# Attention scores from queries and keys that are split into two parts where they are projected

## The chip, the cores and the metric

One core of a Trainium2 chip runs the whole kernel. The metric is the device time of one execution in microseconds (us). The engines named below are TensorE (PE, and PEld for its weight loads), VectorE (DVE), ScalarE (ACT), GpSimd (POOL) and SyncE (SP), whose only work here is to issue DMAs.

## What is computed

The kernel is one transformer layer on 1024 tokens of width 1024: two mixers side by side (an attention with latent projections, and an RWKV-7 recurrence), then a mixture of 32 experts. The change is in the attention, whose reference is, cut to what matters:

```python
MLA_HEADS, QK_NOPE_DIM, QK_ROPE_DIM, V_HEAD_DIM = 8, 64, 32, 64   # QK_HEAD_DIM = 96
def mla_group(p, cos, sin, q_norm_g, w_uq, kv_norm_g, w_uk, w_uv, out_g):
    ...
    q = (rms_norm(q_lat, q_norm_g) @ w_uq).reshape(b, s, MLA_HEADS, QK_HEAD_DIM)
    q = jnp.concatenate([q[..., :QK_NOPE_DIM],
                         rope(q[..., QK_NOPE_DIM:], cos[:, :, None, :], sin[:, :, None, :])], axis=-1)
    c_kv = rms_norm(kv_lat, kv_norm_g)
    k_nope = (c_kv @ w_uk).reshape(b, s, MLA_HEADS, QK_NOPE_DIM)
    v = (c_kv @ w_uv).reshape(b, s, MLA_HEADS, V_HEAD_DIM)
    k_rot = rope(k_rot, cos, sin)
    k = jnp.concatenate([k_nope, jnp.broadcast_to(k_rot[:, :, None, :], (b, s, MLA_HEADS, QK_ROPE_DIM))], axis=-1)
    o = causal_attention(q, k, v)
...
def one_block(args):            # in causal_attention, one block of 128 queries
    scores = jnp.einsum('bqhd,bkhd->bhqk', qb, k, preferred_element_type=jnp.float32) * scale
    scores = jnp.where(k_pos[None, :] <= q_pos[:, None], scores, -jnp.inf)
    probs = jax.nn.softmax(scores, axis=-1).astype(v.dtype)
    return jnp.einsum('bqhk,bkhd->bqhd', probs, v)
```

All inputs and the output are float32.

## The kernel before

**Split products.** Most products of the kernel don't multiply float32 directly. `split` (L204) makes two F32R tiles of a float32 one: `hi`, a copy on ScalarE, and `lo`, the difference, on VectorE. `mm` (L189) then runs three passes into one PSUM bank, at lines L193 (hi by hi), L194 and L195 (the two mixed ones). The attention scores are an exception: L892 is one float32 matmul, which shows as two instructions (x2) in the trace.

**The projections** (`phase_c`, L459, about 100 to 345 us). The float32 tiles of 128 x 1024 that pass through this stage come from `stage`, a ring of 3 buffers (L471). `proj` (L425) and `project` (L546) leave their results in two PSUM banks of the tag `sm`, one for each half of the tokens; `sm` has 4 banks. The main loop takes p = 0 to 3 (called pairs below, since each p gives two heads):

- three calls of `shifted`, which fill one `stage` buffer each with r, k and v of the recurrence and write it to `rkv_d`;
- for p = 0 and 2 `rotary` (L556), which makes the rotated rows of four heads in two `stage` buffers t1 and t2 and writes t1 to `q_d` in four DMAs (L565);
- `nope` (L567) twice, for the 64 unrotated rows of q and of k: one `stage` buffer, two ScalarE copies out of PSUM, two DMAs (L572) to `q_d` or `k_d`;
- two products with `uv` that give the values, copied out (L593) and written to `v_d` (L594).

Between them the loop takes pieces of other work: rows of the adaLN modulation (`mod`, DMAs at L384) and normalized residual rows (`xr`, L410 and L414). After pair 2 the first steps of a recurrence unit are put in.

**The mixers** (`mixers`, L951, about 345 to 820 us) run the eight attention heads beside the units of the recurrence: `head(u)` is a generator that gives way after blocks of queries, and `go(u)` takes one more step of unit u. `mla_setup` (L853) makes two persistent pairs of tiles Q and K, for even and for odd heads, of 128 partitions, of which 96 to 127 are set to zero by four memsets on POOL and 64 to 95 of K hold the rotated key `kr_d`, loaded once. `head` (L870) loads Q and the unrotated part of K in two DMAs (L876, L877), and then, for each of 8 blocks of 128 queries, computes the scores against the keys up to the diagonal in stretches of at most 512 columns (`ms`, 3 banks), adds the mask by a small bf16 matmul (L894), takes the maximum on VectorE, the exponential on ScalarE, and multiplies by the values. So a head has scores of 128, 256, 384 and 512 columns for blocks 0 to 3, and for blocks 4 to 7 one of 512 and one of 128, 256, 384 and 512.

**The order of the work.** The program's text doesn't fix it. The kernel is built with `TileContext(nc, schedule_with_timeline_sim=True)` (L1798): a scheduler places the instructions on each engine's queue, from dependences, buffers and its own estimate of times, and an engine then runs its queue in order. All DMAs named here are issued from SP's queue, in order, and an instruction of SP that waits for data or for a free buffer holds up those behind it.

**The experts** (about 1000 to 2460 us) follow; in them the change moves nothing on TensorE.

The lines that matter for the steps are L471 (ring), L556 to L572 (`rotary`, `nope`), L853 to L877 (`mla_setup`, loads of a head) and L892 (score).

Of the kernel before, what the change touches and what calls it, by code (L numbers as in the profile page):

```python
# [10 lines left out]
F32 = mybir.dt.float32  # L11
F32R = mybir.dt.float32r
# [7 lines left out]
P = 128  # L20
T = 1024
# [142 lines left out]
class Build:  # L164
# [49 lines left out]
    def setup(self):  # L214
        nc, tc, ctx = self.nc, self.tc, self.ctx
        cp = self.cp = ctx.enter_context(tc.tile_pool(name="const", bufs=1))
        self.vecs = cp.tile([P, NV], F32, name="vecs")
        nc.sync.dma_start(self.vecs, self.i["vec"])
        self.csts = cp.tile([P, NC_ALL], F32, name="csts")
        nc.scalar.dma_start(self.csts, self.i["cst"][:, 0:NC_ALL])  # L220
        self.ident = self.cst("ident")
        self.ones = cp.tile([P, P], F32, name="ones")
        nc.vector.memset(self.ones, 1.0)
        eps = cp.tile([P, 4], F32, name="eps")
        for j, v in enumerate((1e-5, 1e-6, 64e-5, 1e-24)):
            nc.gpsimd.memset(eps[:, j:j + 1], v)
        self.eps_ln, self.eps_rms, self.eps_gn, self.eps_kk = (eps[:, j:j + 1] for j in range(4))
        self.dx = ctx.enter_context(tc.tile_pool(name="dram", bufs=1, space=bass.MemoryType.DRAM))
        dram = lambda n, sh: self.dx.tile(sh, F32, name=n)

        self.h2_d = dram("h2_d", [T + P, D])
        self.y_d = dram("y_d", [T + P, D])
        self.mod_d = dram("mod_d", [4, D])
        self.rkv_d = dram("rkv_d", [4, 3, P, T])
        self.sg_d = dram("sg_d", [NB, P, 512])
        self.q_d = dram("q_d", [NH, 96, T])
        self.k_d = dram("k_d", [NH, 64, T])
        self.kr_d = dram("kr_d", [32, T])
        self.v_d = dram("v_d", [NB, P, 512])
        self.ab_d, self.t0_d, self.t0t_d = ([dram(f"{n}{u}", [16, 4160]) for u in range(2)] for n in ("ab_d", "t0_d", "t0t_d"))  # L240
        self.xr_d = dram("xr_d", [T, D])
        self.bs_d = dram("bs_d", [NE, 8, 512])
        self.stats = cp.tile([P, NB, 2], F32, name="stats")
# [215 lines left out]
    def phase_c(self, st, keep, rw_stack):  # L459
# [50 lines left out]
        for h, sl in enumerate(halves):  # L510
            V.tensor_mul(t1[0:32, sl], pp[h][0:32], cos[0:32, sl])
            V.tensor_mul(t2[0:32, sl], pp[h][32:64], sin[0:32, sl])
            V.tensor_add(t1[0:32, sl], t1[0:32, sl], t2[0:32, sl])
        nc.sync.dma_start(self.kr_d, t1[0:32])
        norm(slice(2, 3), "kvg", 128)
        qn, kn = nrm[0:2], nrm[2]
        mod()
# [38 lines left out]
        def rotary(g):  # L556
            pr = project("w_uq", 512 + g * P, qn)
            pw = project("w_uq", 768 + g * P, qn)
            t1, t2 = stage(), stage()
            for h, sl in enumerate(halves):  # L560
                V.tensor_mul(t1[:, sl], pr[h], cos[:, sl])
                V.tensor_mul(t2[:, sl], pw[h], sin[:, sl])
                V.tensor_add(t1[:, sl], t1[:, sl], t2[:, sl])
            for j in range(4):
                nc.sync.dma_start(self.q_d[4 * g + j, 64:96], t1[32 * j:32 * j + 32])  # L565

        def nope(name, p, srcs, dst):  # L567
            t = stage()
            for h, pq in enumerate(project(name, p * P, srcs)):
                S.copy(t[:, halves[h]], pq)  # L570
            for h in range(2):
                nc.sync.dma_start(dst[2 * p + h, 0:64], t[h * 64:h * 64 + 64])  # L572

        uv = self.split_tile(wp, [P, 512], "uv")
        wv = stage()[:, 0:512]
# [2 lines left out]
        for p in range(4):  # L578
# [16 lines left out]
            if p == EARLY_UNIT:  # L595
                for _ in (*mods, *xrows):
                    pass
                smr.close()
                self.rw = self.pool(rw_stack, "rw")
                self.unit_consts()  # L600
                self.unit(0)


    def psum(self, tag, bufs):
# [248 lines left out]
    def mla_setup(self, st):  # L853
        nc = self.nc
        kp = self.pool(st, "kp", side="right")
        self.ap = self.pool(st, "ap", bufs=2, side="right")

        self.Q, self.K = ([kp.tile([P, T], F32, name=f"{n}{j}") for j in range(2)] for n in "QK")
        for t in self.Q + self.K:
            nc.gpsimd.memset(t[96:P], 0.0)  # L860
        for K in self.K:
            nc.sync.dma_start(K[64:96], self.kr_d)
        self.nmask = kp.tile([P, P], BF16, name="nmask")
        self.identb = kp.tile([P, P], BF16, name="identb")
        nc.vector.tensor_copy(self.identb, self.ident)
        nc.gpsimd.memset(self.nmask, 0.0)
        nc.gpsimd.affine_select(self.nmask, self.nmask, [[-1, P]], ALU.is_ge, NEG, base=0, channel_multiplier=1)
        self.vp = None

    def head(self, h, oT):  # L870
# [1 line left out]
        nc, ap = self.nc, self.ap  # L872
        V, S, mm = nc.vector, nc.scalar, nc.tensor.matmul
        half, other = (slice(64 * j, 64 * j + 64) for j in (h % 2, 1 - h % 2))
        Q, K = self.Q[h % 2], self.K[h % 2]
        nc.sync.dma_start(Q[0:96], self.q_d[h])  # L876
        nc.sync.dma_start(K[0:64], self.k_d[h])  # L877
        if h % 2 == 0:
            self.vp = ap.tile([P, NB, P], F32, name="vp", bufs=1)
            nc.sync.dma_start(self.vp, self.v_d[:, :, h * 64:h * 64 + P].rearrange("b p c -> p b c"))  # L880
# [2 lines left out]
        for qb in range(NB):  # L883
# [4 lines left out]
            for j, c in enumerate(range(0, n, 512)):  # L888
                w = min(n - c, 512)
                s = self.psum("ms", 3)[:, 0:w]  # L890
                last = c + w == n
                mm(s, Q[:, qb * P:(qb + 1) * P], K[:, c:c + w], start=True, stop=not last)  # L892
                if last:
                    mm(s[:, w - P:w], self.identb, self.nmask, start=False, stop=True)  # L894
                V.reduce_max(mx[:, j:j + 1], s, axis=AX.X)
# [906 lines left out]
```

## Time and profile before

| | |
|---|---|
| Runs of the kernel (median; lowest to highest) | 2455.2 us (2453.6 to 2470.61) |
| The profiled execution, its own time | 2466.53 us |
| Its span in the trace | 2464.7 us |
| Mean granted TensorE clock | 0.954 of full speed |
| PE busy | 2286.7 us (93%) |
| PEld busy | 1940.2 us (79%) |
| DVE busy | 1996.8 us (81%) |
| ACT busy | 1409.1 us (57%) |
| POOL busy | 549.3 us (22%) |
| Moved by DMA | 567.80 MB |

Busy times are sums over one execution, so they are averages over stages with different limits: what a stage waits for has to be read in that stage. The profiled execution is one among several and lay 11 us above the median of the others; durations come from it, and a time for the changed kernel has to be set against the runs.

### The profile page before, as it was taken

The numbers are of one execution on the slowest core, as the hardware profiler recorded it, in microseconds if no ns is written. First come the engines' busy times: TensorE is split into PE (matmuls) and PEld (weight loads), VectorE is DVE, ScalarE is ACT, GpSimd is POOL, SyncE is SP. The second block draws the span as 40 slices with busy tenths as digits, with TensorE's granted clock in tenths as the row PEclk, the third lists the DMA queues.
The fourth block names the chain that finished last, engine by engine and source line by source line (L and its number), as shares of the span: only waits on it lengthen the run. The fifth ranks groups of instructions, "written<-read, shape, count | busy, mean of one in ns | idle before, by whom it ended". The sixth has DMA issues, their size and how long they took to land. (4 is left out here: it accounts for less than half of the span.)

```text
span 2464.7 us, 42046 instructions
## 1 busy us (share of the span) xinstructions
PE 2286.7 (93%) x15539; PEld 1940.2 (79%) x15539; DVE 1996.8 (81%) x3878; ACT 1409.1 (57%) x2355; POOL 549.3 (22%) x411
## 2 busy tenths in 40 slices
PE   6999989999998995899999999999999999999992
PEld 3776766676765784888898998989889898888981
DVE  7666447777776776788898989898989898898977
ACT  5333335455545433666676767676667676666764
POOL 1005222222213533121211212111212121111113
PEclk9999989999898995999999999999999999999996
DMA  6378542212123323978898979897979898888973
GB/s 268 119 263 278 187 112 56 59 45 58 34 41 90 115 96 128 342 283 290 297 335 296 338 288 337 281 358 275 363 252 336 297 334 302 292 326 300 333 272 139
DMA packets 167335, 567.80 MB, mean 230 GB/s; under 512 B 64617, under 2 KB 79738, under 8 KB 116821
## 3 DMA queue, kind: packets, MB, share of 16 engines
q1 hardware_dynamic: 155476, 524.63, 58.2%
q0 software_dynamic: 11216, 39.34, 6.5%
q8 instruction: 124, 2.03, 0.3%
q10 hardware_dynamic: 432, 1.09, 0.1%
q14 instruction: 87, 0.70, 0.1%
HBM read 508.22 MB, written 56.79 MB: 229 GB/s over the span
## 5 line engine op out<-in xcount | busy, mean ns | idle before, releaser
L206 DVE TENSOR_TENSOR wsl<-w,wsh 128x1024 fp32r<-128x1024 f32 x786 | 932.9, 1218 | 143.6 <-ACT wsh L205 142.1
L205 ACT CAST wsh<-w 128x1024 fp32r<-128x1024 f32 x786 | 782.8, 1047 | 346.6 <-PE acc L195 91.9
L193 PE MATMUL acc<-wsh,xTh 128*128 128x256 f32 x1344 | 381.9, 285 | 10.0 <-ACT xTh L205 5.1
L1525 PE MATMUL acc<-xw,wsh 128*128 128x368 f32 (+7 forms) x1408 | 381.1, 354 | 8.0 <-DVE t L1530 8.0
L194 PE MATMUL acc<-wsl,xTh 128*128 128x256 f32 x1344 | 382.9, 285 | 0.7 <-DVE wsl L206 0.7
L195 PE MATMUL acc<-wsh,xTl 128*128 128x256 f32 x1344 | 381.7, 285 | 0.3 <-DVE xTl L206 0.3
L1527 PE MATMUL acc<-xw,wsl 128*128 128x184 f32 (+7 forms) x1408 | 337.9, 240 | 0.0
L1525 PEld LDWEIGHTS acc<-xw,wsh 128*128 128x128 f32 x1408 | 268.9, 191 | 10.1 <-issue 5.4
L1527 PEld LDWEIGHTS acc<-xw,wsl 128*128 128x128 f32 x1408 | 273.3, 194 | 0.7
L193 PEld LDWEIGHTS acc<-wsh,xTh 128*128 128x128 f32 x1344 | 258.5, 193 | 13.2 <-ACT xTh L205 7.0
L194 PEld LDWEIGHTS acc<-wsl,xTh 128*128 128x128 f32 x1344 | 259.4, 193 | 4.8 <-DVE wsl L206 1.0
L195 PEld LDWEIGHTS acc<-wsh,xTl 128*128 128x128 f32 x1344 | 259.2, 193 | 1.8 <-DVE xTl L206 0.6
L1459 POOL DMA_INDIRECT y_d<-y,idx x42 | 143.0, 3405 | 420.5 <-DVE y L1451 333.3
L1362 POOL DMA_INDIRECT xg<-h_d,idx x43 | 97.7, 2273 | 615.7 <-issue 272.2
L193 PE MATMUL acc<-wsh,uTh 128*128 128x512 f32 x512 | 203.5, 400 | 19.2 <-ACT uTh L205 19.2
L194 PE MATMUL acc<-wsl,uTh 128*128 128x512 f32 x512 | 202.4, 396 | 0.0
L195 PE MATMUL acc<-wsh,uTl 128*128 128x512 f32 x512 | 193.6, 406 | 1.3 <-DVE uTl L206 1.3
L193 PEld LDWEIGHTS acc<-wsh,uTh 128*128 128x128 f32 x512 | 97.3, 190 | 40.7 <-ACT uTh L205 21.8
L193 PE MATMUL sm<-hTh,wsh 128*128 128x512 f32 x288 | 115.0, 400 | 6.4 <-ACT wsh L205 2.0
L194 PE MATMUL sm<-hTl,wsh 128*128 128x512 f32 x288 | 115.6, 401 | 4.2 <-DVE hTl L347 3.1
L195 PE MATMUL sm<-hTh,wsl 128*128 128x512 f32 x288 | 113.5, 395 | 0.0
L194 PEld LDWEIGHTS acc<-wsl,uTh 128*128 128x128 f32 x512 | 97.8, 191 | 19.3 <-DVE wsl L206 0.2
(584 smaller groups left out, 4323.5 us busy)
## 6 DMA issues: line engine op xcount, KB each, us to landing
w<-in_w_dram SPq DMA_DIRECT2D x384, 1024.0 KB
aw<-in_ada_dram SPq DMA_DIRECT2D x34, 512.0 KB
w<-in_w_in_dram SPq DMA_DIRECT2D x18, 512.0 KB
aw<-in_ada_dram SPq DMA_DIRECT2D x7, 1024.0 KB
rkv_d<-stage SPq DMA_DIRECT2D x12, 512.0 KB
xt<-in_x_dram SPq DMA_DIRECT2D x8, 512.0 KB
xr<-in_x_dram SPq DMA_DIRECT2D x8, 512.0 KB
xr_d<-xr SPq DMA_DIRECT2D x8, 512.0 KB
```

Source lines behind the costliest of these rows:

```text
L193: mm(out, a.hi, b.hi, start=start, stop=False)
L194: mm(out, a.hi, b.lo, start=False, stop=False)
L195: mm(out, a.lo, b.hi, start=False, stop=stop)
L205: (hi_eng or self.nc.scalar.copy)(dst.hi, src)
L206: (lo_eng or self.nc.vector).tensor_tensor(dst.lo, src, dst.hi.bitcast(F32), ALU.subtract)
L1362: self.nc.gpsimd.indirect_dma_start(out=xg[0:n], out_offset=None, in_=self.h2_d, in_offset=bass.IndirectOffsetOnAxis(ap=idx[0:n, 0:1], axi ...
L1459: nc.gpsimd.indirect_dma_start(out=self.y_d, out_offset=bass.IndirectOffsetOnAxis(ap=idx[0:n, 0:1], axis=0), in_=y[0:n], in_offset=None, c ...
L1525: nc.tensor.matmul(acc[:, 0:2 * cap], w.hi[:, c], xw[:, k].rearrange("p a t -> p (a t)"), start=(k == 0), stop=False)
L1527: nc.tensor.matmul(acc[:, 0:cap], w.lo[:, c], xw[:, k, 0], start=False, stop=(k == KD - 1))
```

## The change

It does five things.

1. After the rotation, q and kr are split: `parted` copies t1 into t2 as F32R on ScalarE and leaves the difference in t1 on VectorE, both in place. Both tiles are then written to memory.
2. `nope` takes two `stage` buffers in place of one and splits the two PSUM banks into them: ScalarE copies the high part, VectorE subtracts for the low one.
3. `q_d`, `k_d` and `kr_d` have a leading axis of 2, high and low.
4. The persistent Q and K tiles, their memsets and the single loads of `kr_d` go. Each head loads both parts of Q and K in two halves of 512 tokens, into tiles of 96 x 2 x 512 with two buffers per name: three DMAs for each half (q, k, and the rotated rows of k).
5. A score is three F32R passes in place of one float32 matmul.

```diff
@@ in setup
-        self.q_d = dram("q_d", [NH, 96, T])
-        self.k_d = dram("k_d", [NH, 64, T])
-        self.kr_d = dram("kr_d", [32, T])
+        self.q_d = dram("q_d", [2, NH, 96, T])
+        self.k_d = dram("k_d", [2, NH, 64, T])
+        self.kr_d = dram("kr_d", [2, 32, T])
@@ in phase_c
-        nc.sync.dma_start(self.kr_d, t1[0:32])
+        for part, t in enumerate(self.parted(t1[0:32], t2[0:32])):
+            nc.sync.dma_start(self.kr_d[part], t)
@@ in rotary
-            for j in range(4):
-                nc.sync.dma_start(self.q_d[4 * g + j, 64:96], t1[32 * j:32 * j + 32])
+            for part, t in enumerate(self.parted(t1, t2)):
+                for j in range(4):
+                    nc.sync.dma_start(self.q_d[part, 4 * g + j, 64:96], t[32 * j:32 * j + 32])
@@ in nope
-            t = stage()
-            for h, pq in enumerate(project(name, p * P, srcs)):
-                S.copy(t[:, halves[h]], pq)
-            for h in range(2):
-                nc.sync.dma_start(dst[2 * p + h, 0:64], t[h * 64:h * 64 + 64])
+            th, tl = stage(), stage()
+            for sl, pq in zip(halves, project(name, p * P, srcs)):
+                self.split(Split(th[:, sl].bitcast(F32R), tl[:, sl].bitcast(F32R)), pq)
+            for part, t in enumerate((th, tl)):
+                for h in range(2):
+                    nc.sync.dma_start(dst[part, 2 * p + h, 0:64], t[h * 64:h * 64 + 64])
@@ new
+    def parted(self, x, hi):
+        self.split(Split(hi.bitcast(F32R), x.bitcast(F32R)), x)
+        return hi, x
@@ in mla_setup
-        self.Q, self.K = ([kp.tile([P, T], F32, name=f"{n}{j}") for j in range(2)] for n in "QK")
-        for t in self.Q + self.K:
-            nc.gpsimd.memset(t[96:P], 0.0)
-        for K in self.K:
-            nc.sync.dma_start(K[64:96], self.kr_d)
@@ in head
-        Q, K = self.Q[h % 2], self.K[h % 2]
-        nc.sync.dma_start(Q[0:96], self.q_d[h])
-        nc.sync.dma_start(K[0:64], self.k_d[h])
+        parts = lambda d: d.rearrange("a r t -> r a t")
+        Q, K = [], []
+        for sl in (slice(0, 512), slice(512, T)):
+            q, k = (ap.tile([96, 2, 512], F32R, name=n, bufs=2) for n in "QK")
+            nc.sync.dma_start(q.bitcast(F32), parts(self.q_d[:, h, :, sl]))
+            nc.sync.dma_start(k[0:64].bitcast(F32), parts(self.k_d[:, h, :, sl]))
+            nc.sync.dma_start(k[64:96].bitcast(F32), parts(self.kr_d[:, :, sl]))
+            for t, ts in ((q, Q), (k, K)):
+                ts.append(Split(t[:, 0], t[:, 1]))
...
-                mm(s, Q[:, qb * P:(qb + 1) * P], K[:, c:c + w], start=True, stop=not last)
+                q, k = Q[qb // 4][:, qb % 4 * P:(qb % 4 + 1) * P], K[j][:, 0:w]
+                mm(s, q.hi, k.hi, start=True, stop=False)
+                mm(s, q.hi, k.lo, start=False, stop=False)
+                mm(s, q.lo, k.hi, start=False, stop=not last)
```

Over the whole program, TensorE's 96 float32 score matmuls become 288 F32R ones. VectorE gets 16 more subtractions of 128 x 512, two of 128 x 1024 and one of 32 x 1024; ScalarE two more copies of 128 x 1024 and one of 32 x 1024; POOL loses four memsets of 32 x 1024; SP issues 1333 DMAs in place of 1278.

The lines of the changed kernel lie some 4 to 13 lower down in the text: L568 is the rotary write, L576 the write of `nope`, L883 to L885 the loads of a head, L903 to L905 the three passes.

SP's queue in pair 0 of the projections, before, from the load of the weights for k's `nope` to the first write of the values:

```order
L539 DMA wb<-in_w_uk_dram 128x128
L384 DMA aw_1879<-in_ada_dram 128x1024
L572 DMA q_d<-stage 64x1024 x2
L414 DMA xr_d<-xr 128x1024
L410 DMA xr<-in_x_dram 128x1024
L565 DMA q_d<-stage 32x1024 x4
L572 DMA k_d<-stage 64x1024 x2
L594 DMA v_d<-stage 128x512
```

The same place of the changed kernel:

```order
L576 DMA q_d<-stage 64x1024 x2
L415 DMA xr_d<-xr 128x1024
L568 DMA q_d<-stage 32x1024 x2
L411 DMA xr<-in_x_dram 128x1024
L568 DMA q_d<-stage 32x1024 x6
L411 DMA xr<-in_x_dram 128x1024
L399 DMA mod_d<-ab_1912 1x512
L385 DMA aw_1987<-in_ada_dram 128x1024
L385 DMA aw_1991<-in_ada_dram 128x1024
L541 DMA wb<-in_w_uq_dram 128x2x128 x2
L692 DMA v<-rkv_d 128x512
L576 DMA q_d<-stage 64x1024 x2
```

The rotary rows are now eight writes with the load of an `xr` row among them, and the second part of q's `nope` goes out (last row, behind the weights' loads) well after the first; k's four writes follow it.

SP's queue in the mixers around a head's loads, before; `t_d` and `t0t_d` carry blocks of a unit's triangular solve through memory, `ap` is a block read back for it, `sg` and `r` are inputs of a unit:

```order
L775 DMA t_d_82<-tp 64x16x16
L775 DMA t0t_d_84<-tm 64x16x16
L777 DMA t_5169<-t_d_82 64x8x64 x2
L777 DMA t0t<-t0t_d_84 64x8x64 x2
L876 DMA Q_2540<-q_d 96x1024
L877 DMA K_2542<-k_d 64x1024
L683 DMA r<-rkv_d 128x512
```

The changed kernel at a head's loads:

```order
L757 DMA ap<-ab_d_80 64x16x16
L884 DMA K<-k_d 64x2x512
L885 DMA K<-kr_d 32x2x512
L883 DMA Q<-q_d 96x2x512
L884 DMA K<-k_d 64x2x512
L885 DMA K<-kr_d 32x2x512
L690 DMA sg<-sg_d 128x4x128
L784 DMA t_d_82<-tp 64x16x16
L784 DMA t0t_d_84<-tm 64x16x16
```

Two DMAs have become six, of which five stand here; `ap` is right ahead of them and the stores of the triangular solve behind them.

TensorE's queue where head 2 ends and head 3 begins, before:

```order
L892 MATMUL ms<-K_2541,Q_2539 128x512
L894 LDWEIGHTS identb
L894 MATMUL ms<-nmask,identb 128x128
L892 MATMUL ms<-K_2542,Q_2540 128x128
L894 LDWEIGHTS identb
L894 MATMUL ms<-nmask,identb 128x128
```

And in the changed kernel:

```order
L695 MATMUL s_4131<-csts_92,sg 128x128 x4
L903 MATMUL ms<-K,Q 128x512
L904 MATMUL ms<-K,Q 128x512
L905 MATMUL ms<-K,Q 128x512
L907 LDWEIGHTS identb
L907 MATMUL ms<-nmask,identb 128x128
L903 MATMUL ms<-K,Q 128x128
L904 MATMUL ms<-K,Q 128x128
L905 MATMUL ms<-K,Q 128x128
L907 LDWEIGHTS identb
L907 MATMUL ms<-nmask,identb 128x128
```

In both, the next head's first score stands right behind the last score of the head before. Before, the two read different tiles (K_2541 and K_2542); now both names are K, whose two buffers hold the two halves of one head.

## Rows read from the trace of the kernel before

**Rows 1.** Windows by stage: window, us, busy PE, PEld, DVE, ACT, POOL, PEclk, DMA, GB/s.

```profile
580.00:660.00 80.00, 78.03 (x725) 55.80 (x721) 57.31 (x177) 37.38 (x88) 19.96 (x29) 0.94 0.19 43
...
1100.00:2460.00 1360.00, 1290.51 (x8922) 1184.02 (x8920) 1228.16 (x1967) 907.96 (x1391) 263.33 (x97) 0.98 0.83 303
```

**Rows 2.** Windows, 4 us in pair 0 of the projections.

```profile
196.00:200.00 4.00, 4.00 (x14) 3.16 (x14) 4.00 (x7) 1.60 (x4) 0.57 (x1) 0.69 0.91 263
```

**Rows 3.** Timeline of TensorE, projections: start, us, engine, line, operation, out<-in [idle before].

```profile
200.94 0.40 PE L194 MATMUL sm<-hTl,wsh 128*128 128x512 f32 x1
201.17 0.39 PE L195 MATMUL sm<-hTh,wsl 128*128 128x512 f32 x1
```

**Rows 4.** Timeline of TensorE, experts.

```profile
1500.00 0.28 PE L193 MATMUL acc<-wsh,xTh 128*128 128x256 f32 x1
1500.12 0.28 PE L194 MATMUL acc<-wsl,xTh 128*128 128x256 f32 x1
```

**Rows 5.** Timeline of TensorE, mixers, scores and what follows them.

```profile
602.32 0.70 PE L892 MATMUL ms<-K,Q 128*128 128x256 f32 x2
602.86 0.22 PE L894 MATMUL ms<-nmask,identb 128*128 128x128 bf16 x1
602.91 1.08 PE L892 MATMUL ms<-K,Q 128*128 128x512 f32 x2
603.92 1.09 PE L805 MATMUL s<-gk,t 64*64 64x128 f32 x16
...
608.26 0.81 PE L892 MATMUL ms<-K,Q 128*128 128x384 f32 x2
608.91 0.22 PE L894 MATMUL ms<-nmask,identb 128*128 128x128 bf16 x1
...
609.41 1.02 PE L892 MATMUL ms<-K,Q 128*128 128x512 f32 x2
610.27 1.02 PE L839 MATMUL s<-oc,cen 128*128 128x512 f32 x2
...
621.09 2.08 PE L892 MATMUL ms<-K,Q 128*128 128x512 f32 x2
622.95 0.31 PE L894 MATMUL ms<-nmask,identb 128*128 128x128 bf16 x1
```

**Rows 6.** Timeline of SP (SPq): DMAs issued in the projections and before the first head.

```profile
198.85 1.16 SPq L572 DMA_DIRECT2D q_d<-stage  x2
...
202.50 3.22 SPq L565 DMA_DIRECT2D q_d<-stage  x4
...
288.21 1.87 SPq L565 DMA_DIRECT2D q_d<-stage  x4
...
340.36 0.47 SPq L877 DMA_DIRECT2D K<-k_d  x1
```

**Rows 7.** Timeline of ScalarE, projections.

```profile
204.58 0.59 ACT L593 COPY stage<-sm 128x512 f32<-128x512 f32 x1 [3.35 <-DMA q_d<-stage]
...
222.46 1.05 ACT L205 CAST wsh<-w 128x1024 fp32r<-128x1024 f32 x1 [4.47 <-PE sm L194]
...
244.35 0.59 ACT L593 COPY stage<-sm 128x512 f32<-128x512 f32 x1 [2.38 <-DMA rkv_d<-stage]
```

**Rows 8.** Timeline of VectorE, the last add of `rotary` in pair 0.

```profile
199.11 0.68 DVE L563 TENSOR_TENSOR stage<-stage 128x512 f32<-128x512 f32 x1
```

**Rows 9.** Timeline of TensorE, pairs 0, 1 and 2 and the first score.

```profile
198.85 0.39 PE L193 MATMUL sm<-uvh,nrm2h 128*128 128x512 f32 x1
...
243.78 0.50 PE L193 MATMUL sm<-hTh,wsh 128*128 128x512 f32 x1
...
289.56 0.39 PE L193 MATMUL sm<-uvh,nrm2h 128*128 128x512 f32 x1
...
346.33 2.90 PE L892 MATMUL ms<-K,Q 128*128 128x128 f32 x6 [3.34 <-DMA K<-k_d]
```

**Rows 10.** Waits of SP's queue, 340 to 900 us: instruction <- cause: us, count, longest.

```profile
SPq L748 <- DMA ab_d<-lt: 19.3, 7, 6.8
```

## The prediction

> **What bounds the kernel now.** I read the windows by stage first. Between 580 and 660 us, in the mixers, TensorE is busy 78.0 of 80 us, VectorE 57.3 and the DMA engines 0.19 of the time [rows 1]; in the experts (1100 to 2460) TensorE holds 1290.5 of 1360 us. No instruction of the experts moves, so the change shows in the projections (100 to 345 us) and in the mixers (345 to 820), and in both TensorE's own time and what holds it up count. The second view is TensorE's timeline, read by starts: a row's duration contains the way through the array, so the cost of a matmul is the distance to the next start. The third is the timelines of SP, ScalarE and VectorE around the first pair's `nope`, where the stage buffers go round.
>
> **The passes.** Before, one 512-wide score is two rows and lasts from 602.91 to 603.92 (1.01 us), or 0.86 (609.41 to 610.27) where the next matmul's weights come easily; 384 wide 0.65 (608.26 to 608.91), 256 wide 0.54 (602.32 to 602.86) [rows 5]. At half clock a 512-wide one takes 1.86 (621.09 to 622.95) [rows 5]. The three-pass form stands elsewhere in this kernel: 512 columns start every 0.23 us (200.94, 201.17) [rows 3], 256 every 0.12 (1500.00, 1500.12) [rows 4]; so a score becomes 0.68 us at 512, about 0.52 at 384 and 0.36 at 256. 128 wide I take as half of 256, on both sides. There are 8 heads with 6 scores of 512 and 2 each of the other widths. Before: 48 x 1.01 + 16 x (0.65 + 0.54 + 0.27) = 72 us, and some 7 us for the eight or so that run at half clock: 79. After: 48 x 0.68 + 16 x (0.52 + 0.36 + 0.18) = 50, and 5 for the half clock: 55. That is a saving of 24 at most; with 0.86 for every 512-wide one and no half clock it is 48 x 0.86 + 23 - 50 = 14. I take 20, nearer to the row that most scores look like. TensorE is nearly full in the mixers, but heads 0 and 7 wait for other engines (VectorE's recurrences), so I let three quarters reach the end: **-15 us** (bounds -24 to -10).
>
> A pass more means a weight load more per score. [rows 3] have one load per matmul and still step by 0.23 us, 512 columns at 2.4 GHz being 0.213 of it: the load is hidden. The Trainium skill ("TensorE: Matmul & The Clock Gate", section "LDWEIGHTS (loading the stationary operand)") gives a load as columns over 1.2, which is 0.107 us for 128 columns. By that, unhidden, 96 more loads would be an estimated 10 us and the saving half as large; the rows speak against it here. Rival 4 prices the same mechanism from a row.
>
> **The stage ring.** `stage` has 3 buffers, `sm` 4 banks. Before, `nope` takes one buffer and lets a bank go at ScalarE's copy. Now it takes two, and a bank goes only when VectorE has subtracted into the second. In pair 0 the third `shifted` buffer is free, the other two are `rotary`'s t1 and t2, and both of these are now written to memory (before, t2 was free at the last add). So the first half's bank waits for a rotary buffer to land. Step by step: last add ends at 199.8 [rows 8]; the high copy of 128x1024 costs 1.05 [rows 7], 200.9; the four DMAs of the high part cost SP 0.8 each (3.22 for 4 [rows 6]) and in the new order an `xr` load stands between them, so they are out at about 205; the q_d writes of before were out at 200.0 [rows 6] and ScalarE waited for them till 204.58 [rows 7], 4.6 us with the DMA engines 0.91 busy [rows 2]; I take 4, so 209; the subtraction 0.65 (an add over 512 is 0.68 [rows 8]), 209.7. TensorE wants that bank for `uv` at 198.85 [rows 9]. `q` and `k` hold all four banks, and the scheduler lets no `hT` matmul go ahead of `uv`. **Pair 0: 10.5 us idle.** Pair 2: SP needs only 0.47 per rotary DMA (1.87 for 4 [rows 6]), TensorE wants the bank at 289.56 [rows 9]; 288.2 (SP sends the finished rotary [rows 6]) + 1.05 + 1.9 + 4 + 0.65 = 295.8: **6 us**. Pairs 1 and 3 have no rotary; there the third `shifted` write holds up `k`, as it held up ScalarE's copy till 244.35 [rows 7]; its low half is done at about 246.5, and TensorE wants the bank at 243.78 [rows 9]: **2.5 us each**. Together 21.5. Behind a short wait TensorE ran at 0.69 of its clock in this stretch [rows 2] and got 14 matmuls (3.2 us' worth by 0.23) into 4 us; two long waits make some 3 us of that. **+24 us.** Below, if other work fills the gaps and buffers land at once, only some 2 us remain (the 16 added subtractions, 16 x 0.65 = 10 us, lie on a VectorE that has room outside these places); above, each of the eight `nope` calls could wait 5 us: 40.
>
> The Trainium skill ("DMA: Bandwidth & Descriptors", section "Anatomy of one DMA — SWDGE (gpsimd) path") fits a DMA as 2.0 us and bytes over 436 GB/s, 2.3 us for 128 KB. By it pairs 0 and 2 would wait an estimated 1.7 us less each and the result would be 3 us lower; the row of 4.6 us, on a loaded queue and another path, decides.
>
> **Loads of the heads.** At the start, pair 3 writes 1 MB more ahead of the first Q and K; at 263 GB/s [rows 2] that is 4 us, of which the missing memsets and the shorter first load give some back: TensorE, which waited till 346.33 for K [rows 9], waits **+2 us** more (0 to 6). Then, Q and K had one buffer for even and one for odd heads and were loaded a whole head ahead. Now the first key half has a buffer of its own that the last block of the head before still reads, and the next head's first score comes right behind that block. Between its last read and that score lie some 40 TensorE instructions, about 5 us (16 of L805 are 1.09 [rows 5], the second 512-wide score 0.68, the rest by their kind). The load needs 5.5 us where the queue is full (issued 340.83, waited for till 346.33 [rows 6, 9]). Behind it on SP stand its rotary half, `sg` and the stores of the unit's triangular solve. A short transfer on a quiet queue hides, a full one costs about a microsecond: 0 to 1.5 us at each of seven boundaries; I take **+4 us** (0 to 12). POOL's four memsets go and were hidden.
>
> **Sum.** -15 + 24 + 2 + 4 = +15 us. The profiled execution lasted 2466.5 (span 2464.7), which would give 2481.5; it stands 11 us above the median 2455.2 of the runs, so the forecast against that is **2470**.
>
> **Rivals.**
> 1. *The ring costs little*: the rotary buffers land early, TensorE waits 5 us in the projections, keys are always in time, the whole 20 us of the scores counts: 5 + 1 - 20 = -14, **2441**. For it: SP's later rotary DMAs cost half of the first ones [rows 6], so the queue is not full everywhere. Against: [rows 2, 7], with ScalarE already waiting for these buffers.
> 2. *Slower, the key hand-over*: in SP's order the key load stands behind `ab_d` and `ap`, and `ap` waits for `ab_d` to land, 19.3 us over 7 times [rows 10], 2.8 each. If that comes after the last read of the keys, a boundary costs 2.8 + 0.6 + 5.5 - 5 = 3.9 us, seven are 27 instead of 4: +38, **2493**. It decides once `ap` is issued later than the last block's first score. For: SP is one queue, and the new K waits on TensorE itself. Against: the unit's step that writes `ab_d` stands well ahead of that score on TensorE, and its wait can end before.
> 3. *All of the score's rows count and the slow-clock stretches go with them*: -24 and another -10, the ring small: **2425**.
> 4. *The loads show*: 96 more of them at the 0.133 us that one holds the load path (1184.02 over 8920 [rows 1]) are 13 us, the saving 7, three quarters of it -5: +25, **2480**. For it: the scores' weights change with each third pass. Against: [rows 3]. The Trainium skill's figure, above, is its neighbour.
>
> **How the numbers follow.** Forecast 0.45; rival 1 0.20; rival 2 0.20; rival 4 0.10; rival 3 0.05. One per cent, 24.6 us, is about what a measurement of this kernel tells from no change. Above 2479.8: rival 2 nearly whole, half of rival 4 and a slice of the forecast, 0.31. Below 2430.7: rival 3, 0.04. Within: 0.65. The extremes of the terms reach from 2433 to over 2500; eight in ten lie in 2443 to 2494; the forecast's own range is 2458 to 2482.
>
> **What would show it.** Right: in the projections TensorE idle before `uv` of pairs 0 and 2 for 10 and 6 us, released by VectorE's subtraction; scores of 512 at 0.23 us per pass; the first score of a head waiting about a microsecond for K. Wrong: if the stretch from 100 us to the first score is less than 10 us longer, the ring term falls; if the mixers are not 8 us shorter, the scores' term does; if K waits add up to over 20 us, rival 2 is it.

## The result and the profile after

The changed kernel takes 2481.01 us (median of seven executions, 2479.01 to 2494.37) against 2456.05 of the kernel before: ratio 1.0101, 95% interval 1.008 to 1.0122, some 25 us slower. An eighth execution took 3671.91 us at a granted clock of 0.55 and is left out; with it the median is 2484.76. The forecast was 2470 in a range of 2443 to 2494. The profiled execution lasted 2494.37 (span 2492.6).

Windows by stage of the changed kernel, with the columns of [rows 1]. The edges are events: from 100 us to the first `uv` product of pair 3, from there to the first score, from there to the first product with `w_o`; last the experts.

```profile
100.00:360.60 260.60, 232.65 (x988) 178.90 (x988) 143.65 (x232) 82.07 (x119) 52.67 (x35) 0.94 0.61 207
360.60:378.70 18.10, 9.55 (x51) 5.85 (x49) 6.58 (x20) 4.43 (x8) 3.65 (x5) 0.62 0.82 234
378.70:833.60 454.90, 433.58 (x3902) 330.86 (x3902) 324.19 (x1069) 232.31 (x535) 113.75 (x166) 0.90 0.29 70
1120.00:2480.00 1360.00, 1298.63 (x9026) 1191.95 (x9024) 1240.42 (x1981) 919.17 (x1404) 270.41 (x97) 0.98 0.84 306
```

The same three stages before:

```profile
100.00:334.00 234.00, 224.86 (x984) 173.89 (x983) 130.50 (x214) 79.15 (x116) 52.98 (x33) 0.99 0.61 212
334.00:346.30 12.30, 7.28 (x51) 4.52 (x49) 5.13 (x19) 4.24 (x8) 7.62 (x11) 0.82 0.99 253
346.30:801.70 455.40, 433.46 (x3811) 306.54 (x3811) 328.85 (x1071) 232.52 (x536) 114.36 (x167) 0.92 0.24 55
```

The projections are 26.6 us longer, the stretch up to the first score 5.8, the mixers 0.5 shorter. TensorE does nearly the same number of instructions in the projections (988 and 984) with 8 us more of busy time and 19 us more of waiting. The granted clock, the column behind POOL's, fell in all three stages. A clock of 0.90 over 454.9 us means that the engine got 409 us' worth at full speed; before, 0.92 of 455.4 made 419. TensorE stands idle for 21 and 22 us of the two stages, so its work in the mixers did fall by about 10 us, and the clock took it back.

TensorE's timeline of the changed kernel, in the projections; in brackets what it waited for:

```profile
209.07 1.86 PE L397 MATMUL md<-acc,ones 128*1 128x512 f32 x2 [5.16 <-DVE acc L391]
216.28 0.80 PE L193 MATMUL sm<-uvh,nrm2h 128*128 128x512 f32 x1 [5.34 <-DVE stage L206]
...
262.81 0.79 PE L193 MATMUL sm<-nrm2h,wbsh 128*128 128x512 f32 x1 [5.67 <-DVE stage L446]
...
322.36 0.50 PE L193 MATMUL sm<-hTh,wsh 128*128 128x512 f32 x1 [0.74 <-DVE stage L206]
```

And VectorE's, at the first of those waits for a subtraction:

```profile
210.98 0.68 DVE L398 TENSOR_TENSOR ab<-md,ab 1x512 f32<-1x512 f32 x1 [1.96 <-PE md L397]
215.54 1.29 DVE L206 TENSOR_TENSOR stage<-sm,stage 128x512 fp32r<-128x512 f32 x2 [3.88 <-DMA q_d<-stage]
```

This is the chain of the stage ring: `uv` of pair 0 (before at 198.85 [rows 9]) waits for the low part, and that for a rotary buffer to land. But half of pair 0's 10.5 us is a wait for `acc`, the sum of the modulation, and pair 1's 5.67 us is a wait for a `shifted`: neither is the ring, and pair 2 hardly waits. From `uv` to `uv`, the change adds 17.4 us up to pair 0, 7.3 from there to pair 1, 4.5 to pair 2 and takes 2.7 on the way to pair 3.

TensorE's timeline of the changed kernel around two scores:

```profile
445.19 0.50 PE L903 MATMUL ms<-K,Q 96*128 96x512 f32 x1
445.53 0.39 PE L904 MATMUL ms<-K,Q 96*128 96x512 f32 x1
445.76 0.39 PE L905 MATMUL ms<-K,Q 96*128 96x512 f32 x1
446.00 0.60 PE L768 MATMUL s<-csts,xa 128*128 128x128 f32 x4
...
449.03 0.33 PE L903 MATMUL ms<-K,Q 96*128 96x128 f32 x1
449.19 0.28 PE L904 MATMUL ms<-K,Q 96*128 96x128 f32 x1
449.31 0.28 PE L905 MATMUL ms<-K,Q 96*128 96x128 f32 x1
449.42 0.23 PE L907 MATMUL ms<-nmask,identb 128*128 128x128 bf16 x1
```

A score of 128 columns before:

```profile
442.55 0.39 PE L892 MATMUL ms<-K,Q 128*128 128x128 f32 x2
442.78 0.22 PE L894 MATMUL ms<-nmask,identb 128*128 128x128 bf16 x1
```

Read by starts, 512 columns take 0.34, 0.23 and 0.24 us, 0.81 in all, and 128 columns 0.16, 0.12 and 0.11: 0.39 in place of 0.23, where the forecast had 0.68 and 0.18. All scores together, by starts, took 80.4 us before and 76.8 after; counted at full clock, 72.0 and 65.8.

The first score of all waited longer (3.34 us for K in [rows 9]); no later head's first score waits for a key at all:

```profile
378.74 0.45 PE L903 MATMUL ms<-K,Q 96*128 96x128 f32 x1 [5.54 <-DMA K<-kr_d]
```

### The profile page after: what moved, and what is told of

It is laid out like the page before. It is cut to its first block, busy times and chain, and to the rows that moved or that the text cites. A ratio compares the mean times of both kernels' runs of the same rounds, so it can differ in the third digit from the quotient of the medians.

```text
span 2492.6 us, 42377 instructions
## 1 busy us (share of the span) xinstructions
PE 2295.6 (92%) x15635; PEld 1968.1 (79%) x15635; DVE 2010.5 (81%) x3897; ACT 1411.2 (57%) x2358; POOL 546.1 (22%) x407
## 5 line engine op out<-in xcount | busy, mean ns | idle before, releaser
L1540 PE MATMUL acc<-xw,wsl 128*128 128x184 f32 (+7 forms) x1408 | 336.5, 239 | 0.0
```

The source lines that it names most:

```text
L1540: nc.tensor.matmul(acc[:, 0:cap], w.lo[:, c], xw[:, k, 0], start=False, stop=(k == KD - 1))
```

## The experiments

"Last uv" below is the first `uv` product of pair 3, the end of the projections: 334.0 us before, 360.6 after. "Half clock" is the time in which TensorE was granted 1.2 GHz, "full-clock work" a stage's length less half of that (waits are in it). Both are summed here from the trace's own record of the clock; the expectations have the half clock 1 to 3 us lower. Times are against the kernel before on the same chip.

**1. Two more buffers.** In pairs 0 to 2 the low parts of `nope` go into two buffers of a pool of their own.

```diff
+        lp = self.pool(smr, "lp", side="right")
+        low = lambda: lp.tile([P, T], F32, name="low", bufs=2)
-            th, tl = stage(), stage()
+            th, tl = stage(), low() if p <= EARLY_UNIT else stage()
```

> The changed kernel with two buffers of their own for the low parts of nope, in pairs 0 to 2 (pair 3 keeps the ring). Ring theory (the 26.6 us by which the last uv product comes later are waits for buffers of the ring of three, and the low clock behind them): TensorE's waits before uv of pair 0 (5.3 us) and in pair 1 (5.7 us) go, the last uv product comes 15 to 22 us earlier than in the changed kernel, and the time against the kernel before falls from +25 to between +3 and +10 us; what stays is the wait in the first steps (2.5 us near 149 us), pair 3 and the first loads of the heads. Rival (the added work itself: 16 subtractions on VectorE and 6 MB more written beside a loaded queue): the waits keep most of their length under other names, the last uv product comes less than 6 us earlier, the time stays at +19 or more.

Measured: 2483.86 us, ratio 1.0108 (1.0067 to 1.0148). In pair 0 `uv` comes at 204.3 in place of 216.3, so the ring's chain is real; but last uv is at 354.3, 6 us earlier. What came in its place, VectorE's and then TensorE's timeline of this kernel:

```profile
228.65 0.49 DVE L389 TENSOR_SCALAR acc<-aw,cT 128x512 f32<-128x512 f32 x1 [16.79 <-DMA aw<-in_ada_dram]
```

```profile
209.29 1.86 PE L397 MATMUL md<-acc,ones 128*1 128x512 f32 x2 [2.48 <-DVE acc L391]
...
257.84 0.79 PE L193 MATMUL sm<-nrm2h,wbsh 128*128 128x512 f32 x1 [6.84 <-DVE stage L446]
```

The ring alone is not it.

**2. The projections alone.** Mixers of before on the high parts (the low parts of q and k are left out of the scores).

```diff
...
+        nc.sync.dma_start(Q[0:96], self.q_d[0, h])
+        nc.sync.dma_start(K[0:64], self.k_d[0, h])
...
-                mm(s, q.hi, k.hi, start=True, stop=False)
-                mm(s, q.hi, k.lo, start=False, stop=False)
-                mm(s, q.lo, k.hi, start=False, stop=not last)
+                mm(s, Q[:, qb * P:(qb + 1) * P], K[:, c:c + w], start=True, stop=not last)
```

> The changed kernel's projections with the mixers of before: heads load only the high parts into the persistent tiles and multiply them in float32; the low parts are written and not read. Theory (projections and start cost all, the mixers give nothing back): the last uv product comes 26 us later than before, and the whole time is +27 to +33 us, the same as the changed kernel's or up to 5 more. Rival (the passes do save some 15 us, and the new loads take it back): +26 at the last uv product all the same, but the mixers then equal those of before to the microsecond either way, so this run gives the sum of the first two terms; if the time is under +20 the projections' term is smaller than the traces say.

Measured: 2479.54, ratio 1.0076 (1.0052 to 1.0099). Last uv 359.4, first score 376.0, mixers 454.3: the projections and the start cost 25 and 4 us, and without a pass in it the mixers are as long as with them. The whole is some 19 us over before, less than expected: what follows the mixers lasted 1646.5 us in its profile, against 1663.0 and 1653.5 in the two of the kernel before.

**3 and 4. The rows of the tiles.** The changed kernel with tiles of 128 rows, and the kernel before with 96.

```diff
+        self.Q, self.K = ([kp.tile([P, 2, 512], F32R, name=f"{n}{j}") for j in range(2)] for n in "QK")
+        for t in self.Q + self.K:
+            nc.gpsimd.memset(t[96:P].bitcast(F32), 0.0)
...
-            q, k = (ap.tile([96, 2, 512], F32R, name=n, bufs=2) for n in "QK")
...
```

```diff
-                mm(s, Q[:, qb * P:(qb + 1) * P], K[:, c:c + w], start=True, stop=not last)
+                mm(s, Q[0:96, qb * P:(qb + 1) * P], K[0:96, c:c + w], start=True, stop=not last)
```

> The changed kernel with Q and K tiles of 128 rows, the last 32 zeroed once, in place of 96. In the trace of the changed kernel a score's first pass of 512 columns takes 0.32 us to the next start behind a matmul of 128 rows and 128 columns, and 0.336 behind other shapes, where the passes behind it take 0.23; in the trace of before a first float32 pass takes 0.43 behind 128 by 128 and 0.53 behind other shapes. Shape theory (a weight load hides only behind a matmul of the same rows and columns): the first passes behind 128 by 128 fall to 0.23, those behind other shapes stay at 0.33; some 40 of 96 scores, 0.09 each, 3 to 5 us of TensorE, 0 to 5 of the whole time. Rival (the first pass waits for its operands, or a new accumulation costs 0.1): the first passes stay at 0.31 to 0.32 everywhere.

> The kernel before with the float32 score over 96 rows in place of the zero-padded 128. Shape theory: a first float32 pass of 512 columns behind a 128 by 128 matmul goes from 0.43 to 0.52 or 0.53 us, about 20 of the 96 scores and the narrow ones behind the mask likewise, 2 to 5 us of TensorE, 0 to 5 of the whole time. Rival (rows don't matter): 0.43 stays.

Measured: 2486.36 (1.0083 to 1.0143) and 2478.88 (1.0041 to 1.0098). The shape theory fell: with 128 rows the first pass behind 128 by 128 still takes 0.315 us, with 96 rows the first float32 pass still 0.43. (The 0.09 are a matter of where a start is put: the matmul in front then steps by 0.03 in place of 0.11.) But the kernel with 96 rows, in which no duration of a score changed, lost 17 us. Its mixers:

```profile
345.70:821.20 475.50, 448.75 (x3810) 318.32 (x3810) 330.83 (x1071) 232.95 (x536) 119.13 (x169) 0.88 0.24 58
```

As many instructions as before, a full-clock work of 419 us against 418, and 113 us at half clock against 74. The scheduler had put the mixers into another order: compared line by line, 1516 of the 15539 matmuls stand elsewhere than in the trace of before, against 4 between the two traces of the unchanged kernel (number 7). So the mixers' length hangs on the order and on the clock by more than the scores are worth.

**5 and 6. The stores.** Number 5 is number 2 with the low parts computed and not written. Number 6 is number 1 with the stores of the low parts issued by ScalarE.

```diff
...
-            for part, t in enumerate((th, tl)):
+            for part, t in enumerate((th,)):
```

```diff
...
-                    nc.sync.dma_start(dst[part, 2 * p + h, 0:64], t[h * 64:h * 64 + 64])
+                    (nc.sync, nc.scalar)[part].dma_start(dst[part, 2 * p + h, 0:64], t[h * 64:h * 64 + 64])
```

> As the projections alone (mixers of before on the high parts), but the low parts of q, k and kr are computed and not written to memory; nothing reads them. The last uv product came at 360.6 us in the changed kernel, 359.4 with the projections alone, 354.3 with two more buffers, 334.0 before. Store theory (what is left with more buffers is the 6 MB of low-part stores: SP issues them ahead of the modulation weights aw, VectorE waits 16.8 us for those and TensorE behind it): the last uv product comes at 334 to 341 us and the time is within 8 us of before. Compute theory (the added subtractions and copies on VectorE and ScalarE, in order with everything else there): it stays at 350 or later, and the time at +15 or more.

> The changed kernel with the two more buffers for the low parts, and the stores of the low parts of nope and rotary issued from ScalarE's queue in place of SP's. Queue theory (SP's queue is what delays: the stores stand ahead of the loads of aw and w and of the stores that free the ring): VectorE's wait of 16.8 us for aw in pair 1 falls below 8, the last uv product comes 6 us or more earlier than the 354.3 us with two more buffers, and the time is at most +18 us. Volume theory (the DMA engines are full there, 0.9 and more of the time, so 6 MB more take their 20 us whatever queue issues them): the last uv product stays at 351 to 357.

Measured: 2482.48 (1.0059 to 1.0131), last uv 355.7; 2500.85 (1.0101 to 1.0192), last uv 364.2. The store theory fell: without a single low store the projections are 4 us shorter than in number 2. ScalarE's queue is a worse place for them: VectorE's wait for `aw` did fall, from 16.8 to 6.7 us, but the last uv is later than either theory had it. Number 5 has float32 scores and a mean granted clock of 0.956 over its runs, near that of before; span times clock, what the runs would be worth at full speed, is 2371.7 us against 2357.9, so most of its loss is real work and waiting.

**7 and 8. Both kernels again, for a second profile.**

> The kernel before, unchanged, for a second profile. In the first TensorE ran 73 us of the mixers (346.3 to 801.7) at half clock, in the changed kernel 91, in the kernel with 96 rows 110, with nearly the same work; the work of the mixers counted at full clock was 418.7, 407.9 and 419.9 us. If the half-clock time belongs to the order of the instructions, it is 70 to 77 us here again and the mixers last 453 to 458 us. If it varies from run to run, it differs by 10 us or more, and the mixers' length with it by half of that.

> The changed kernel, unchanged, for a second profile. If the half-clock time of the mixers belongs to the order: 88 to 95 us again, mixers of 452 to 457 us, and the last uv product at 359 to 362. If it varies from run to run: another 10 us or more either way, and then the 10.8 us of full-clock work that the three-pass scores save show in the mixers' length in runs of equal clock.

Measured: 2451.68 and 2488.51, one run each. The mixers of before, then of the changed kernel:

```profile
348.40:796.40 448.00, 422.49 (x3811) 299.34 (x3811) 328.17 (x1072) 232.56 (x536) 115.68 (x168) 0.95 0.24 56
```

```profile
373.60:831.60 458.00, 433.76 (x3902) 329.09 (x3902) 325.55 (x1069) 231.83 (x535) 113.38 (x166) 0.90 0.29 69
```

The half clock of before varies from run to run (74 and 48 us), that of the changed kernel stood at 92 both times. Full-clock work: 418.3 and 424.1 before, 408.9 and 412.2 after. The saving is there in both pairs, 9 and 12 us, though two runs of one kernel differ by up to 6. The mixers are 10.0 us longer in this pair, where they were 0.5 shorter in the first. Last uv 336.5 and 356.2.

**9. The bank let go by ScalarE.** Number 1, but PSUM is copied out by ScalarE as before and split afterwards, low part on GpSimd, so that VectorE does nothing new.

```diff
...
-            th, tl = stage(), stage()
+            tl, th = stage(), low() if p <= EARLY_UNIT else stage()
...
-                self.split(Split(th[:, sl].bitcast(F32R), tl[:, sl].bitcast(F32R)), pq)
+                S.copy(tl[:, sl], pq)
+            self.parted(tl, th)
...
-        self.split(Split(hi.bitcast(F32R), x.bitcast(F32R)), x)
+        self.split(Split(hi.bitcast(F32R), x.bitcast(F32R)), x, lo_eng=self.nc.gpsimd)
```

> The changed kernel with two more buffers for nope (pairs 0 to 2), PSUM let go as before by a plain ScalarE copy, and the split done afterwards from SBUF: high part on ScalarE, low part on GpSimd, in nope, rotary and kr. VectorE does nothing that it did not do before. Order theory (in the changed kernel TensorE's banks are let go by VectorE, whose queue of the modulation work stands ahead; neither the ring nor the stores alone): the waits of TensorE for a stage subtraction are gone, the last uv product comes at 335 to 345 us (334 and 336.5 in the two profiles of before, 354 to 360 in the variants so far), and the time is +5 to +15 us. Rival (any added link between projection and store costs the same: more instructions in the same in-order queues, loads pushed behind): the last uv product stays at 350 to 362, and the time at +20 or more.

Measured: 2498.22 (1.0106 to 1.0181), last uv 350.4. The waits for a stage subtraction are gone, and yet last uv and time are the rival's: the order theory fell. `uv` of pair 0 is at 203.2, nearly where it was before, and most of the loss (12.8 us) lies between pairs 0 and 1, with two waits of TensorE that are not the split's:

```profile
212.49 1.87 PE L397 MATMUL md<-acc,ones 128*1 128x512 f32 x2 [7.21 <-DVE acc L391]
257.84 0.79 PE L193 MATMUL sm<-uvh,nrm2h 128*128 128x512 f32 x1 [4.74 <-DVE stage L446]
```

**10. Split at the load.** Projections of before; a head loads float32 and splits there, so that only the scores and the loads are changed.

```diff
...
+            nc.sync.dma_start(q[:, 1].bitcast(F32), self.q_d[h, :, sl])
+            nc.sync.dma_start(k[0:64, 1].bitcast(F32), self.k_d[h, :, sl])
+            nc.sync.dma_start(k[64:96, 1].bitcast(F32), self.kr_d[:, sl])
+            for t, ts in ((k, K), (q, Q)):
+                s = Split(t[:, 0], t[:, 1])
+                self.split(s, t[:, 1].bitcast(F32), lo_eng=nc.gpsimd)
...
```

> The projections of before, unchanged; q, k and kr are written once, in float32. A head loads them into the low halves of the changed kernel's tiles and splits there: four copies of 96 x 512 on ScalarE and four subtractions on GpSimd per head. The scores are the three passes. Theory (the scores give some 8 to 11 us of TensorE's work at full clock, and TensorE runs longer at half clock with them): last uv product at 333 to 337 us as before; mixers with 406 to 418 us of full-clock work, 85 to 95 us at half clock and 450 to 460 long; time within 8 us of before either way. Rival 1 (the saving is real and was hidden by the worse projections): mixers under 445 us, the time 5 to 15 under before. Rival 2 (the first key half, which now also waits for its split, holds up each head): waits of TensorE for K of over 1 us at most heads, time +10 or more.

Measured: 2481.11, ratio 1.007 (1.0048 to 1.0093). Last uv 337.9, so the projections cost nothing; and yet it is some 18 us slower. Waits for K: 2.3 us, at the first head alone. Rivals 1 and 2 fell, and the theory had the time wrong:

```profile
350.00:831.70 481.70, 444.34 (x3906) 335.33 (x3906) 346.51 (x1071) 248.52 (x566) 157.00 (x200) 0.87 0.22 54
```

It ran 122 us of the mixers at half clock. Against the first profile of before its mixers are 26 us longer: TensorE stands idle for 37 us in place of 22, half clock while it is busy costs 22 us more, and its work, waits left out, is 12 us less at full clock. So by this count the passes save what they save elsewhere, and more waiting and more half clock outweigh it. Over its 12 runs the mean granted clock is 0.947; for the kernel before, 17 runs beside them, 0.958. Span times clock is 2344.5 us against 2353.6: nine less, in a kernel whose span is 18 longer (2476.2 against 2457.7).

**11 and 12. The modulation held.** VectorE's modulation steps may not be issued ahead of the `shifted` that they follow in the text: in the changed kernel, and in number 1. The reason, windows of the modulation's sum alone (`acc`), from `uv` of pair 0 to pair 1 and on to pair 2; DVE is the column that counts. Before:

```profile
198.80:240.80 42.00, 1.02 (x2) 0.09 (x2) 11.21 (x12) 0.00 (x0) 1.00 0.89 306
240.80:289.60 48.80, 2.04 (x4) 0.17 (x4) 11.93 (x8) 0.00 (x0) 1.00 0.58 199
```

The changed kernel:

```profile
216.30:265.50 49.20, 1.02 (x2) 0.09 (x2) 19.08 (x16) 0.00 (x0) 0.88 0.81 282
265.50:318.80 53.30, 1.02 (x2) 0.09 (x2) 0.00 (x0) 0.00 (x0) 0.98 0.61 197
```

The scheduler had moved the modulation forward: the second stretch has none left, and the first has 16 instructions in place of 12. With both edits below, they are 10 and 14.

In the edit, `shifted` returns its last instruction:

```diff
...
-                self.shifted(4 + 4 * j + p, t)
+                behind = self.shifted(4 + 4 * j + p, t)
...
-                mod(MODS)
+                with tc.issue_after(behind.ins):
+                    mod(MODS)
```

> The changed kernel, with one thing fixed in VectorE's queue: the two modulation steps that follow a shifted in the text are issued behind that shifted's last instruction. In the two profiles of before VectorE runs 11 modulation instructions between the first uv product of pair 0 and that of pair 1 and 8 more up to pair 2; in all kernels with changed projections 15 to 18 and 0 to 4, and TensorE waits 2.5 to 7.2 us for the modulation's sum and 4.7 to 9.1 for a shifted of pair 1 there. Modulation theory (a good half of the lost 20 us is that the scheduler pulls this work forward into the gaps which the split leaves, ahead of what lets TensorE's banks go): both waits fall below 2 us, the last uv product comes at 343 to 352 us in place of 356 to 361, the time 5 to 14 us below the changed kernel's. Rival (the waits only move: the ring of three and VectorE's new bank release hold TensorE all the same): the last uv product stays at 354 to 362.

> The same with the two more buffers for the low parts in pairs 0 to 2. Theory (ring and pulled-forward modulation together make the projections' 20 us): the last uv product comes at 336 to 344 us, against 334 and 336.5 before, and the time is +2 to +10 us against before, the rest being the first loads (5 us) and mixers that gain nothing. Rival: what was left with more buffers (354 us) is the added instructions themselves; it stays at 348 or later and the time at +15 or more.

Measured: 2498.8 (1.0112 to 1.0169), last uv 365.9; 2497.27 (1.0117 to 1.0167), last uv 341.9. Held alone it is worse: TensorE's waits for the split's subtractions grow from 7.6 to 15.7 us, and those for the modulation's sum and the `shifted` of pair 1, which it was to remove, stay (5.10 and 8.19). With the buffers as well, TensorE's timeline has left of the three waits of the changed kernel

```profile
203.22 0.79 PE L193 MATMUL sm<-uvh,nrm2h 128*128 128x512 f32 x1 [4.50 <-DVE low L206]
...
247.83 0.50 PE L193 MATMUL sm<-nrm2h,wbsh 128*128 128x512 f32 x1 [1.67 <-DVE stage L446]
```

and of the 20 to 27 us, 5 to 8 stay, with all the added subtractions and stores still in it. So number 11's theory fell, the projections' part of number 12's holds, and the two edits together undo most of the loss of the projections, where neither does alone: 360.6 and 356.2 with both, 354.3 without the ring, 365.9 without the other, 341.9 without either. Each of these kernels has its own order, so the exact link between the two is argued from the queues, not shown. The time did not follow: +2 to +10 us was expected and the ratio 1.0142 is some 35. In the profile the mixers of number 12 last 471.3 us, with 93 at half clock and 425 of full-clock work, in an order of their own. No version of these beats the kernel before.

## Why the prediction was right, and where it was wrong

The range held the time and the sign was right, but the sum of +15 is made of terms whose errors partly cancel, so that the hit is in part luck: the forecast had the scores give more, the clock cost less and the waits cost more than they did. The measured 1.0101 lies on the bound between "same" (0.65) and "slower" (0.31).

1. **The stage ring, +24.** Measured +26.6 and, in the second pair of profiles, +19.7: the right size, by luck in part. The chain worked out for pair 0 is in the trace link by link, its waits of 10.5 us are the 10.5 foreseen, and yet half of them have another cause; pair 2 was given 6 us and waits 0.7, pair 1 was given 2.5 and waits 7.1. The step had TensorE, ScalarE and SP's queue and left out what the scheduler does with VectorE's: once the split opens gaps, the modulation goes into them, ahead of the instructions that let banks go. Number 12 bears it out; number 11 shows that the ring is needed for it.
2. **The start, +2 (0 to 6).** Measured 5.8 and 5.5, at the upper bound: SP's loads of the first head stand behind eight stores of 64 rows instead of four. Numbers 2 and 5 show it, with the mixers of before behind both: the stretch lasts 16.7 us with the low stores and 11.8 without them.
3. **The key hand-over, +4 (0 to 12).** Zero: no head after the first waits for a key in either profile, and rival 2 fell with it.
4. **The scores, -20 on TensorE and -15 at the end: the step that failed.** By the prediction's own sign (mixers 8 us shorter) the term falls: they were 0.5 us shorter and, in the second pair, 10.0 longer. By starts the scores went from 80.4 us to 76.8, and in the second pair from 77.5 to 78.3; at full clock from 72 to 66 in both: 6, not 20, and below the lower bound of 14. The 72 of before is what the forecast had; the passes were given 50 and took 66. Of these 16 us, 9 are in the 512-wide scores, 3 in the narrowest and 4 in the two widths between.
   - The boundaries. The row taken for most scores, 1.01 us, contained 0.05 us on entering, behind the mask, and 0.09 on leaving, where the neighbour's tile has 64 rows (a float32 pass starts 0.43 us before the next between tiles of 128 by 128, 0.53 behind a 64-row or 64-column one). The passes pay at both ends again: the 512-wide scores of the changed kernel take 0.86 us in the mean at full clock, not 0.68. At best, between tiles of 128 by 128, they take 0.77 to 0.78, of which 0.08 comes back in the shorter step of the matmul in front; counted with such steps, the saving is some 8 us in place of 6.
   - The narrow scores. "128 wide I take as half of 256" has a floor: a pass of 128 columns steps by 0.11 us, not 0.06, so a narrow score rose from 0.22 to 0.37 (medians at full clock). This is rival 4's mechanism, a load that shows, if it is the weight load that sets this step; no run here separates that. The Trainium skill ("TensorE: Matmul & The Clock Gate", section "LDWEIGHTS (loading the stationary operand)") gives a load as columns over 1.2, an estimated 0.107 us for 128 columns; the step of 0.112 lies near it.
5. **The clock, some 3 us in the forecast: the largest miss.** The seven runs of the changed kernel had a mean granted clock of 0.949 on a span of 2482.9 us; the 18 runs of the kernel before that stand beside numbers 1 to 4 had 0.958 on 2458.6 (of those beside the result the clocks are not on record). Span times clock is 2355.2 and 2355.4 us, as if the clock were all. But this product counts a wait at half clock as half its length, which hides 6 us of the waits that the change adds, and it sets the rest of them off against the work that was saved. In the two pairs of profiles, whose spans differ by 27.9 and 36.8 us, TensorE's idle time (span less PE busy) is 19 and 17 us longer, where the forecast had 27.5; half clock while it is busy costs 17 and 30 us more, where it had 3; its work at full clock is 8 and 10 us less, where it had 15. The half-clock time grew from 3 and 14 us to 31 and 34 in the projections, behind the long waits, and from 74 and 48 to 92 in the mixers.

What stays open is why TensorE's clock falls more often in the mixers with the passes: 87 to 123 us in eight of nine profiles with them (69 with 128 rows), 37 to 74 in four of five with float32 scores (113 with 96 rows). It is not waiting alone: in the changed kernel the clock fell around 692 us behind a stretch in which TensorE was busy throughout,

```profile
686.00:692.00 6.00, 6.00 (x58) 4.84 (x55) 4.92 (x15) 2.93 (x7) 3.75 (x6) 1.00 0.26 46
692.00:697.00 5.00, 5.00 (x27) 3.77 (x27) 0.61 (x3) 0.60 (x2) 0.00 (x0) 0.57 0.14 14
```

and every experiment also changed the order, so passes and order were not told apart.

## What to carry to other kernels

Price a matmul by the distance between starts, at each width that occurs and beside the neighbours that it will have: a cost that belongs to the boundary stays when the form changes. A step that takes one more buffer of a ring also moves what a scheduler puts into the gap; look at the queue of the engine that lets the banks go, with the new order in hand. Before a difference of one per cent is explained, multiply span by granted clock, and take the idle time apart first: here equal products stood for 17 to 19 us more waiting and 8 to 10 us less work.

## What was not expected

An edit that changed no duration (96 rows for 128) cost 17 us, in another order of the mixers and with a mean granted clock of 0.950 in place of 0.958; span times clock is 2352.3 us against 2355.4. The same program's mixers had 74 and 48 us of half clock in two runs. And a kernel worth 9 us less by span times clock (number 10) ran 18 us longer.
